# Second layer of a two-layer decoder on 1088 instead of 1104 columns: four slices of 272, no attention of the 16 meta queries, a residual tile of its own

## The chip, the cores and the metric

One Trainium2 chip, one core. The metric is the device time of one execution in microseconds (us). The core has a matrix engine (TensorE: PE, with its weight loads shown apart as PEld), a vector engine (VectorE: DVE), an engine for activation functions (ScalarE: ACT), a general engine (GpSimd: POOL) and a synchronising engine (SyncE: SP), which here does nothing but issue DMAs. Each engine runs its own instructions in program order and waits on semaphores for what the others make. A DMA issued from an engine stands in that engine's order too: where it must wait, everything behind it waits.

## The reference

One inference step of a decoder with two layers. Two groups of requests run through the same weights: one prompt of 1024 tokens, with 16 learned meta tokens ahead of it, and 8 samples of 8 new tokens each. The first layer is an mLSTM with state, the second an attention whose scores get a cumulative log-forget value per row (FoX). Keys, values and forget values come from the output of the first layer. Each layer is followed by a SwiGLU FFN (1024 to 2 x 2816 to 1024).

```
h = h + mlstm_mixer(rmsnorm(h, norm_a), ...);  h = h + swiglu(rmsnorm(h, norm_ffn[0]), ...)
k, v, lf = shared_kv(h, ...)                      # all 16 + 1024 rows of the prompt, 64 of the samples
h = h + fox_mixer(rmsnorm(h, norm_b), (k, v, lf)) # queries, gate, attention, w_out
h = h + swiglu(rmsnorm(h, norm_ffn[1]), ...)
y = rmsnorm(h, norm_final);   y_prompt = yp[:, N_META:]
```

Outputs are `y_prompt`, `y_sample`, the states and the keys, values and forget values (those of the meta tokens among them). Behind the keys and values the rows of the meta tokens reach no output: the last line drops them, and other rows' attention uses only their keys and values.

## The kernel before

**Columns.** The residual lies transposed: 1024 features as 8 blocks (`KT`) of 128 partitions, tokens as columns. There are `T` = 1104 columns: 64 of the samples (`NS`), 16 meta (`NM`), together `T0` = 80, and 1024 of the prompt. For the layers' large products they are cut into four slices `TS` of `SL` = 276 columns. Weights are the stationary operand, 128x128 each, and a slice streams past them. Every fp32 product is made of three matmuls (`mm3`, L193 to L195: high part by high, low part by high, high by low), so a 128x128 block against one slice is three matmuls of 276 columns.

**Stages of the second layer** (times in the profile):
- Sample attention, to about 1730 us: eight batches in `attend_sample` on POOL, ACT, DVE and PE. Between its small PE products stand the matmuls of the query gate (tile `bps`, 384 or 336 columns); `f(n)` puts n steps of them at a place. The order of PE is that of the code.
- The attention of the 16 meta queries, L2696 to L2731, behind the eighth batch: two groups of 8 heads. For each group SP issues 16 small loads of forget values (`nm`, `cm`), DVE adds the row mask `m16` to `nm`, POOL lays the queries out (`qmt`), PE makes the scores (`mps`, four matmuls), ACT the softmax, PE the transpose and the value products (`pom`), DVE the copy into `yS`. `m16` is made at the start of the kernel by `row_mask`.
- Prompt attention, `attend_prompt`, to 1978 us: scores `sp`, softmax, values, for 8 head pairs. The masks `nd` are made on POOL, and DVE's custom instruction adds them to the scores. Meanwhile the gate of the last head pair leaves as `ogb` to the DRAM tile `og2D`. `ys` and `first_tile` hold the 80 columns of samples and meta tokens.
- `mlp`: the output projection, `unit(t, m)` for four slices and 8 blocks m of 128 features: 24 matmuls into a PSUM tile `pops` (pool of four), then DVE adds it to the residual `Ht` (L535), then ACT squares it for the norm. The residual is loaded by SP from the DRAM tile `hD` (L499), slice by slice, among the loads of w_out (L518); DVE and ACT split the weights into high and low parts (`split`, L271 and L272).
- The FFN's first half: pairs of slices and of weight halves go through a Strassen-like scheme with seven products (`product`, L1650, tiles `m`), 22 units. DVE makes the sums and differences.
- The FFN's second half: seven rounds of down products (`dps`, L1989), then `Tail.finish` (L2116) and the final norm and transposes, `final` and `turn`.

**The norm.** `root` (L364) sums squares over partitions by tiny matmuls with one column: chunk by chunk of `NR` = 92 columns, three chunks, two tiles of squares each. A tiny fp32 matmul runs as two passes, so a root is 12 records of PE. ACT takes the root, `diag` (L375) makes a diagonal on DVE, `spread` (L382) spreads it over 128 partitions with one matmul of 276 columns. The second layer does this four times for the FFN's norm.

**What sets the order.** PE's order is that of the code throughout, DVE's and ACT's in the FFN as well; elsewhere a scheduler places DVE, ACT, POOL and SP instructions by their dependences. Many of the meta queries' loads are placed early: `nm` and `cm` stand among the loads of the first sample batches.

Of the kernel before, what the change touches and what calls it, by code (L numbers as in the profile page):

```python
# [32 lines left out]
SL = T // 4  # L33
NR = SL // 3
TS = [(SL * i, SL * i + SL) for i in range(4)]
# [10 lines left out]
NEG = -1.0e30  # L46

# [129 lines left out]
class Net:  # L177
# [19 lines left out]
    def consts(self):  # L197
        nc, I = self.nc, self.I
        c = self.ctx.enter_context(self.pool("const"))
        self.dram = self.ctx.enter_context(self.tc.tile_pool(name="scr", bufs=1, space=DRAM))  # L200
        self.c = c
        self.ident = c.tile([P, P], F32, name="ident")
        make_identity(nc, self.ident)
        self.ones = c.tile([P, P], F32, name="ones")
        nc.vector.memset(self.ones, 1.0)
        self.eps = c.tile([P, 1], F32, name="eps")
        nc.vector.memset(self.eps, EPS)
        self.gain = c.tile([P, NG], F32, name="gain")
        self.ptab = c.tile([1, NB * NPG], I32, name="ptab")
        self.clast = c.tile([P, 1], F32, name="clast")  # L210
        rm = c.tile([P, P], F32, name="rowm")
        self.q8, self.m16 = rm[:, :NQ], rm[:, NQ : NQ + NM]
        with self.pool("g0") as gp, self.pool("g0p", space=PSUM) as pp:
            rows = gp.tile([8, P], F32, name="grows")
            nc.scalar.dma_start(rows, I["norm_a"][0].rearrange("(k p) -> k p", p=P))
            nc.scalar.activation(self.clast, self.eps, AF.Sqrt)
            ps = pp.tile([P, 8], F32, name="gps")
            nc.tensor.transpose(ps, rows, self.ident[:8, :8])
            nc.vector.tensor_copy(self.gain[:, G_A : G_A + 8], ps)
# [106 lines left out]
    def place(self, nm):  # L326

        self.turn[nm] += 1
        a = ("ns", "nq", "nf").index(nm) * 2 * SL + self.turn[nm] % 2 * (SL if nm != "nf" else 4)
        return self.sq[:, a : a + (SL if nm != "nf" else 4)]  # L330

    def add_sq(self, H, t, m, sp, x, late=KT - 1):

        nc = self.nc
        t0, t1 = TS[t]
        n = t1 - t0
# [20 lines left out]
    def root(self, t, pp, **kw):  # L357

        nc = self.nc
        self.settle()  # L360
        ps = pp.tile([P, 512], F32, name=self.uid("nps"), **(kw or {"tag": "n"}))
        for c in range(3):
            for j, s in enumerate(self.sums[t]):
                nc.tensor.matmul(ps[:NR, c : c + 1], s[:, NR * c : NR * c + NR], self.ones[:, :1], start=j == 0,  # L364
                                 stop=j == 1)
        f = self.place("nf")[:NR]
        nc.scalar.activation(f[:, :3], ps[:NR, :3], AF.Sqrt, scale=1.0 / D, bias=self.eps[:NR])
        return [ps, f]

    def diag(self, st):  # L370

        nc, f = self.nc, st[1]
        nc.vector.reciprocal(f[:, :3], f[:, :3])
        d = self.place("nq")[:NR].rearrange("p (c n) -> p c n", c=3)
        nc.vector.tensor_tensor(out=d, in0=self.ident[:NR, :NR].unsqueeze(1).broadcast_to([NR, 3, NR]),  # L375
                                in1=f[:, :3].unsqueeze(2).broadcast_to([NR, 3, NR]), op=ALU.mult)
        st.append(d)

    def spread(self, st, r):

        nc, (ps, _, d) = self.nc, st
        nc.tensor.matmul(ps[:, :SL], self.ones[:NR], d.rearrange("p c n -> p (c n)"), start=True, stop=True)  # L382
        nc.scalar.copy(r, ps[:, :SL])

# [7 lines left out]
    def norm_jobs(self, H, t, g, r, pp=None):  # L392

        nc = self.nc
# [43 lines left out]
    def run(self):  # L438
# [6 lines left out]
        with ExitStack() as c1:  # L445
            xp = c1.enter_context(self.pool("x"))
            self.xs = [xp.tile([P, KT, PX + T], F32R, name=f"x{s}")[:, :, PX:] for s in "hl"]
            self.X, self.XG = ([tuple(x[:, :, a:b] for x in self.xs) for a, b in at] for at in (TS, TG))
            with ExitStack() as c2:
# [4 lines left out]
                H = [vt[:, KT * a : KT * b].rearrange("p (k n) -> p k n", k=KT) for a, b in TS]  # L454
# [6 lines left out]
            ys = yp.tile([P, KT, T0], F32, name="yS")  # L461
# [3 lines left out]
            cy.close()  # L465
            hp = c1.enter_context(self.pool("H"))
            self.H = hp.tile([P, KT, T], F32, name="Ht")
            H = [self.H[:, :, a:b] for a, b in TS]
            raws = [tuple(self.H[:, :, b : b + P] for b in (a, a + P)) for a in (0, 2 * P)]
            self.nr = hp.tile([P, SL], F32, name="nr")  # L470
            self.w2 = self.H[:, :2, :512]
            self.mlp(H, raws, I["w_out_b"][0], 1)

    def mlp(self, H, raws, w, l, heads=None, cb=None):

        nc = self.nc
        E = mybir.EngineType
        fixed, order = ExitStack(), ExitStack()
        self.sums = {}
        with self.pool(self.uid("nsp")) as sp, self.pool(self.uid("npp"), bufs=2, space=PSUM) as pn:  # L480
# [14 lines left out]
            with ExitStack() as c:  # L495
# [3 lines left out]
                load = lambda e, t: e.dma_start(H[t], self.hD[:, :, TS[t][0] : TS[t][1]])  # L499
# [26 lines left out]
                def unit(t, m, x):  # L526
# [10 lines left out]
                    if t % 2:  # L537
                        nc.gpsimd.dma_start(self.hD[:, m, TS[t][0] : TS[t][1]], H[t][:, m])
                    elif x == KT - 1:
                        nc.gpsimd.dma_start(self.hD[:, :, TS[t][0] : TS[t][1]], H[t])  # L540
# [77 lines left out]
    def turned(self, pool, nm):  # L618

        return {x: tuple(pool.tile([P, 4, SL], F32R, name=f"T{nm}_{x}{s}") for s in "hl") for x in (2, 1, 4)}  # L620
# [11 lines left out]
def values_a(self, v, kp, gates, w_in, c3):  # L632
# [9 lines left out]
    with ExitStack() as cw, self.pool("ppA0", bufs=4, space=PSUM) as pp:  # L642
# [205 lines left out]
        for n, dst in ((NQ, self.q8), (NM, self.m16)):  # L848
            self.row_mask(kp.tile([P, P // n, n], F32, name=self.uid("rm"), tag="rm"), dst, n)
# [751 lines left out]
def ffn(self, H, l, weights, order, TA, pn, pair, each, early, end=None):  # L1601
# [3 lines left out]
    nc, I = self.nc, self.I  # L1605
    E = mybir.EngineType
# [9 lines left out]
    with self.pool(f"ffn{l}") as fp, self.pool(f"ffnp{l}", space=PSUM) as pp:  # L1616
# [253 lines left out]
        with fixed(E.DVE, E.Activation):  # L1870
# [90 lines left out]
            for i, (hs, z, c) in enumerate(seq if each else seq[:-2]):  # L1961
# [18 lines left out]
                for m, h in [(m, h) for h in hs for m in range(4)] if apart else [(m, h) for m in range(4) for h in hs]:  # L1980
# [13 lines left out]
                    if last:  # L1994
# [3 lines left out]
                        if z in whole:  # L1998
                            t, y = whole[z]
                            if apart:  # L2000
                                square(2 * h + t - 1, 4 * y + m)
                                if m == 3:
                                    s = 2 * h + t - 1
                                    nc.scalar.dma_start(self.hD[:, :, TS[s][0] : TS[s][1]], H[s])
# [16 lines left out]
                for y, k in home[i] if i < len(home) else ():  # L2021
                    nc.gpsimd.dma_start(H[y][:, k : k + 2], self.hD[:, k : k + 2, TS[y][0] : TS[y][1]])
# [18 lines left out]
class Tail:  # L2041


    def __init__(self, net, fp, bank, pn, place):
        self.net, self.bank, self.pn = net, bank, pn
        self.at = TT[DONE[3][0]][0]
        self.sum = place[:, : T - self.at]
        self.last = net.slots[0][:, : T - self.at]
        self.tmp = [net.nr, fp.tile([P, SL], F32, name="tq")]
# [7 lines left out]
    def square(self, t, m, a=None, b=None, keep=False):  # L2057
        nc = self.net.nc
        a, b = a or max(TS[t][0], self.at), b or TS[t][1]
# [18 lines left out]
    def turn(self, ps, i, k):  # L2078
        self.net.nc.tensor.transpose(ps[:, k % 4 * P : k % 4 * P + P], self.net.H[:, k, slice(*TT[i])], self.net.ident)

    def second(self):
        nc = self.net.nc
        nc.vector.memset(self.last[:, : TS[3][0] - self.at], 0.0)
# [24 lines left out]
    def finish(self, acc, groups):  # L2108
        net = self.net
        nc, H = net.nc, net.H  # L2110
        for m in range(4):
            o = acc[m, 1][:, :SL]
# [4 lines left out]
            y = H[:, m, TS[3][0] :]  # L2117
# [14 lines left out]
def final(self, t, fp, pools):  # L2132

    nc, O = self.nc, self.O
    pp, pn = pools
# [371 lines left out]
def sample_masks(self, sp):  # L2507
# [15 lines left out]
    return dm, self.m16, qb  # L2523
# [23 lines left out]
def attend_sample(self, sk, sp, s2, pp, cq, ncn, masks, Y, fill):  # L2547
# [4 lines left out]
    dm, m16, qb = masks  # L2552
# [143 lines left out]
    vm = sp.tile([NM, D], F32, name="vmS", tag="vnS")  # L2696
    nc.sync.dma_start(vm, self.vD[:NM])
    for g in range(2):
        nm = sp.tile([P, NM], F32, name=f"nm{g}")
        cm = sp.tile([P, 1], F32, name=f"cm{g}")  # L2700
        for h in range(8):
            hh = 8 * g + h
            nc.sync.dma_start(nm[h * NM : (h + 1) * NM], self.cD[hh, :NM].partition_broadcast(NM))
            nc.sync.dma_start(cm[h * NM : (h + 1) * NM], self.cD[hh, :NM].unsqueeze(1))
        nc.vector.tensor_tensor(out=nm, in0=nm, in1=m16, op=ALU.add)
        Q = sp.tile([P, 4, P], F32, name=f"qmt{g}", tag="qmt")
        nc.gpsimd.memset(Q, 0.0)
        for j in range(4):
            for z in range(2):
                r = slice(z * 64, z * 64 + 64)  # L2710
                nc.gpsimd.tensor_copy(Q[r, j, (2 * j + z) * NM : (2 * j + z + 1) * NM], qt[r, 4 * g + j, NS:])
        pn = pp.tile([P, 512], F32, name=f"mps{g}", tag="sn", bufs=1)
        for j in range(4):
            nc.tensor.matmul(pn[:, :NM], Q[:, j, :], kt[:, 4 * g + j, NS:], start=(j == 0), stop=(j == 3))
        s = s2.tile([P, NM], F32, name=f"sM{g}", tag="sM")
        mx = s2.tile([P, 2], F32, name=f"mxM{g}", tag="mx")
        nc.vector.tensor_tensor_reduce(out=s, in0=pn[:, :NM], in1=nm, scale=1.0, scalar=NEG, op0=ALU.add,
                                       op1=ALU.max, accum_out=mx[:, 0:1])
        f(6)
        self.softmax_rows(s2, s, NM, mx[:, 0:1], cm, "S", 2)  # L2720
        nc.tensor.transpose(pn[:NM, 64 : 64 + P], s, self.ident)
        pt = s2.tile([NM, P], F32, name=f"ptM{g}", tag="ptM")
        nc.vector.tensor_copy(pt, pn[:NM, 64 : 64 + P])
        f(3)
        po = pp.tile([P, 4, 32], F32, name=f"pom{g}", tag="po", bufs=1)
        for j in range(4):
            nc.tensor.matmul(po[:, j, :], vm[:, (4 * g + j) * P : (4 * g + j + 1) * P], pt[:, j * 32 : j * 32 + 32],
                             start=True, stop=True)
        for z in range(2):
            r = slice(z * 64, z * 64 + 64)  # L2730
            nc.vector.tensor_copy(Y[r, 4 * g : 4 * g + 4, NS:T0], po[r, :, z * NM : z * NM + NM])  # L2731
# [11 lines left out]
def attend_prompt(self, ys):  # L2743
# [3 lines left out]
    with self.pool("ap", bufs=1) as sp, self.pool("ap2", bufs=2) as s2, self.pool("app", bufs=2, space=PSUM) as pp:  # L2747
# [25 lines left out]
        def first_tile():  # L2773

            og0 = w7f[1][:, : KT * T0].rearrange("p (k n) -> p k n", k=KT)
            nc.sync.dma_start(og0, self.og2D[:, :, :T0].rearrange("m p t -> p m t"))
            yield
            nc.vector.tensor_tensor(out=ys, in0=ys, in1=og0, op=ALU.mult)
            self.split(ys, *(x[:, :, :T0] for x in self.xs))
# [302 lines left out]
```

## Time and profile before

| | us |
|---|---|
| median of three runs | 2812.15 |
| lowest, highest | 2809.46, 2819.71 |
| the profiled run | 2814.68 |
| its span (first to last instruction) | 2813.1 |

The profiled run is 1.6 us longer than its span. The granted TensorE clock was 0.995 of full speed over the run.

The page gives busy time by engine, the span in 40 slices, and the costliest groups of instructions. A group's row is line, engine, operation, tile out<-tile in, shapes and count, then busy time, mean length, and idle time just before. Matmuls overlap: records of PE are longer than the step from one to the next. In rows by time the first number is the start in us from the span's start, the second the length; in square brackets stands how long the engine was idle before, and for whom. A window's row is its bounds and length, then busy time and instructions of the engines asked for, the granted clock, the DMA engines' share and GB/s.

The DMA engines by slices of 1/40 of the span (busy tenths, then GB/s):

```profile
DMA  7666555355564375545443775532524555527556
GB/s 214 174 184 175 154 158 196 108 154 157 175 177 137 119 248 172 189 146 166 145 167 131 257 278 207 170 128 87 158 86 130 176 176 162 162 91 233 185 190 220
```

### The profile page before, as it was taken

Reading aid. Unit: us, or ns where it says so; the run is one execution under the profiler, and the core shown is the slowest. Engines: PE = TensorE matmul, PEld = TensorE weight load, DVE = VectorE, ACT = ScalarE, POOL = GpSimd, SP = SyncE. Lnnn points to the kernel's source line nnn. Section 1 sums busy time; section 2 is a strip of 40 time slices with the busy share of each in tenths; the row PEclk is TensorE's granted clock in tenths of the full one; section 3 lists DMA queues with packets and bytes.
Section 4 is the critical chain, followed back from the end, with each engine's and each line's share of the span. In section 5 each row is a group of like instructions: output and inputs, shape, how many; then the busy total and the mean of one; then the engine's idle time right before and its main releaser. Section 6 shows DMA issues by size and latency. Waiting matters only on the chain. (4 is left out here: it accounts for less than half of the span.)

```text
span 2813.1 us, 60646 instructions
## 1 busy us (share of the span) xinstructions
PE 2751.4 (98%) x23543; PEld 2648.8 (94%) x23543; DVE 1793.8 (64%) x4025; ACT 1176.6 (42%) x2299; POOL 855.1 (30%) x1348
## 2 busy tenths in 40 slices
PE   9999989999999999999999999999999999999998
PEld 8999979999999999999999888677999999999998
DVE  5633556888887655662455444776388888765656
ACT  5432553422223334453444445777343223323345
POOL 3142333223223232124452202444313223323111
PEclk9999999999999999999999999999999999999999
DMA  7666555355564375545443775532524555527556
GB/s 214 174 184 175 154 158 196 108 154 157 175 177 137 119 248 172 189 146 166 145 167 131 257 278 207 170 128 87 158 86 130 176 176 162 162 91 233 185 190 220
DMA packets 432419, 474.05 MB, mean 169 GB/s; under 512 B 37014, under 2 KB 358290, under 8 KB 431106
## 3 DMA queue, kind: packets, MB, share of 16 engines
q1 hardware_dynamic: 380562, 320.52, 37.0%
q0 software_dynamic: 44928, 143.44, 15.5%
q10 hardware_dynamic: 6640, 6.21, 0.7%
q8 instruction: 185, 3.03, 0.5%
q14 instruction: 104, 0.85, 0.1%
HBM read 322.84 MB, written 147.21 MB: 167 GB/s over the span
## 5 line engine op out<-in xcount | busy, mean ns | idle before, releaser
L1650 PE MATMUL m<-xh,slot 128*128 128x276 f32 x2752 | 540.6, 290 | 1.9 <-ACT fs L1679 1.8
L1650 PEld LDWEIGHTS m<-xh,slot 128*128 128x128 f32 x2752 | 439.5, 188 | 3.8 <-ACT fs L1679 2.2
L1650 PE MATMUL m<-xl,slot 128*128 128x276 f32 x1376 | 397.0, 289 | 0.0
L1650 PEld LDWEIGHTS m<-xl,slot 128*128 128x128 f32 x1376 | 258.6, 188 | 0.0
L193 PE MATMUL tmps<-slot,xh 128*128 128x256 f32 (+2 forms) x864 | 243.1, 281 | 0.0
L195 PE MATMUL tmps<-slot,xl 128*128 128x256 f32 (+2 forms) x864 | 240.6, 278 | 0.0
L194 PE MATMUL tmps<-slot,xh 128*128 128x256 f32 (+2 forms) x864 | 240.5, 278 | 0.0
L272 DVE TENSOR_TENSOR slot<-slot,slot 128x1024 fp32r<-128x1024 f32 x124 | 162.8, 1313 | 60.7 <-ACT slot L271 59.2
L271 ACT CAST slot<-slot 128x1024 fp32r<-128x1024 f32 x124 | 129.5, 1045 | 143.9 <-PE m L1650 111.7
L194 PEld LDWEIGHTS tmps<-slot,xh 128*128 128x128 f32 (+1 forms) x864 | 159.2, 184 | 0.1
L195 PEld LDWEIGHTS tmps<-slot,xl 128*128 128x128 f32 (+1 forms) x864 | 158.6, 184 | 0.0
L193 PEld LDWEIGHTS tmps<-slot,xh 128*128 128x128 f32 (+1 forms) x864 | 158.4, 183 | 0.2
L193 PE MATMUL mmA<-xh,whi 128*128 128x384 f32 (+1 forms) x384 | 134.6, 350 | 2.9 <-ACT stg L960 2.9
L194 PE MATMUL mmA<-xl,whi 128*128 128x384 f32 (+1 forms) x384 | 128.9, 336 | 0.0
L195 PE MATMUL mmA<-xh,wlo 128*128 128x384 f32 (+1 forms) x384 | 128.7, 335 | 0.0
L272 DVE TENSOR_TENSOR slot<-vA,slot 128x1024 fp32r<-128x1024 f32 (+1 forms) x59 | 82.3, 1397 | 32.7 <-ACT slot L271 31.5
L272 DVE TENSOR_TENSOR slot<-Ht,slot 128x1024 fp32r<-128x1024 f32 (+1 forms) x59 | 82.0, 1393 | 32.7 <-ACT slot L271 31.6
L271 ACT CAST slot<-vA 128x1024 fp32r<-128x1024 f32 (+1 forms) x59 | 60.8, 1035 | 95.7 <-PE m L1650 90.7
L271 ACT CAST slot<-Ht 128x1024 fp32r<-128x1024 f32 (+1 forms) x59 | 60.9, 1036 | 95.5 <-PE m L1650 84.6
L1754 DVE TENSOR_TENSOR ws<-ws 128x128 f32<-128x128 f32 x264 | 93.8, 355 | 8.8
L2904 ACT ACTIVATE s<-s,nb 128x272 f32<-128x272 f32 (+7 forms) x126 | 98.8, 786 | 0.0
L2939 ACT COPY th<-tp 128x768 f32<-128x768 f32 (+1 forms) x80 | 73.5, 919 | 53.5 <-PE tp L2931 30.5
(809 smaller groups left out, 8675.1 us busy)
## 6 DMA issues: line engine op xcount, KB each, us to landing
ws<-in_w_down SPq DMA_DIRECT2D x176, 128.0 KB, 2.7
sD<-ws SPq DMA_DIRECT2D x176, 128.0 KB, 2.1
slot<-sD SPq DMA_DIRECT2D x40, 512.0 KB, 4.0
slot<-in_w_gate_up SPq DMA_DIRECT2D x36, 512.0 KB, 4.0
kp<-in_cache_k SPq DMA_DIRECT2D x32, 512.0 KB, 6.2
vp<-in_cache_v SPq DMA_DIRECT2D x32, 512.0 KB, 5.2
vA<-in_w_gate_up SPq DMA_DIRECT2D x26, 512.0 KB, 4.0
Ht<-in_w_gate_up SPq DMA_DIRECT2D x26, 512.0 KB, 3.9
```

Of the source, the lines that this page charges most:

```text
L193: mm(ps, sh, mh, start=first, stop=False)
L194: mm(ps, sh, ml, start=False, stop=False)
L195: mm(ps, sl, mh, start=False, stop=last)
L271: self.nc.scalar.copy(hi, src)
L272: self.nc.vector.tensor_tensor(out=lo, in0=src, in1=hi.bitcast(F32), op=ALU.subtract)
L1650: nc.tensor.matmul(u.ps[h, b], w[p][:, k], x[q][:, k], start=first and k == i == 0, stop=k == 3 and i == 2, skip_group_check=True)
L1754: tt(out=o, in0=a, in1=b, op=ALU.subtract)
L2904: nc.scalar.activation(ss[z, u], ss[z, u], AF.Exp, bias=nb[:, z : z + 1], accum_out=sm[:, u, z : z + 1])
L2939: nc.scalar.copy(th.rearrange("p x z (u h q) -> p h (x z u) q", h=2, q=64)[:, :, :n], pt[:, :, :n])
```

## The change

A class `Columns` holds the cuts of one layer, and the network holds the current one in `self.cols`. The first layer has 80 + 1024 columns as before (slices of 276, norm in 3 chunks of 92). The second has 64 + 1024 = 1088: slices of 272, norm in 4 chunks of 68. Its x is the same tile read from column 16 on, so the samples' 64 columns move up by 16 behind the keys and values. Its residual in SBUF is 1088 wide. In DRAM it gets a tile `hL`, which `mlp` writes and reloads; the first load still comes from `hD` by a new `load_h`, slice 0 in two pieces (64 and 208 columns), as the meta columns lie between. The loop over the meta queries, its row mask and its value load are deleted. `yS` and `first_tile` have 64 columns.

```diff
+class Columns:
+    def __init__(self, meta, x0):
+        self.T0 = NS + meta
+        self.T = self.T0 + SEQ
+        self.x0 = x0
...
+        self.SL = self.T // 4
+        self.NC = 4 if meta == 0 else 3
+        self.NR = self.SL // self.NC
+        self.TS = [(self.SL * i, self.SL * i + self.SL) for i in range(4)]
+LAYERS = (Columns(NM, 0), Columns(0, NM))
...
-        for c in range(3):
+        NR, NC = self.cols.NR, self.cols.NC
+        for c in range(NC):
             for j, s in enumerate(self.sums[t]):
                 nc.tensor.matmul(ps[:NR, c : c + 1], s[:, NR * c : NR * c + NR], self.ones[:, :1], start=j == 0,
                                  stop=j == 1)
...
+    def columns(self, l):
+        c = self.cols = LAYERS[l]
+        self.X = [tuple(x[:, :, c.x0 + a : c.x0 + b] for x in self.xs) for a, b in c.TS]
+        self.hL = self.hD if l == 0 else self.dram.tile([P, KT, c.T], F32, name="hL")
+    def load_h(self, e, H, t):
+        a, b = self.cols.TS[t]
+        x0 = self.cols.x0
+        if x0 and a == 0:
+            e.dma_start(H[0][:, :, :NS], self.hD[:, :, :NS])
+            a = NS
+        e.dma_start(H[t][:, :, a - self.cols.TS[t][0] :], self.hD[:, :, x0 + a : x0 + b])
...
-                load = lambda e, t: e.dma_start(H[t], self.hD[:, :, TS[t][0] : TS[t][1]])
+                load = lambda e, t: self.load_h(e, H, t)
...
-                        nc.gpsimd.dma_start(self.hD[:, m, TS[t][0] : TS[t][1]], H[t][:, m])
+                        nc.gpsimd.dma_start(self.hL[:, m, TS[t][0] : TS[t][1]], H[t][:, m])
...
-        for n, dst in ((NQ, self.q8), (NM, self.m16)):
-            self.row_mask(kp.tile([P, P // n, n], F32, name=self.uid("rm"), tag="rm"), dst, n)
+        self.row_mask(kp.tile([P, P // NQ, NQ], F32, name=self.uid("rm"), tag="rm"), self.q8, NQ)
...
-    vm = sp.tile([NM, D], F32, name="vmS", tag="vnS")
-    nc.sync.dma_start(vm, self.vD[:NM])
-    for g in range(2):
-        nm = sp.tile([P, NM], F32, name=f"nm{g}")
-        cm = sp.tile([P, 1], F32, name=f"cm{g}")
-        for h in range(8):
-            hh = 8 * g + h
-            nc.sync.dma_start(nm[h * NM : (h + 1) * NM], self.cD[hh, :NM].partition_broadcast(NM))
-            nc.sync.dma_start(cm[h * NM : (h + 1) * NM], self.cD[hh, :NM].unsqueeze(1))
-        nc.vector.tensor_tensor(out=nm, in0=nm, in1=m16, op=ALU.add)
...
-        f(6)
-        self.softmax_rows(s2, s, NM, mx[:, 0:1], cm, "S", 2)
...
-            nc.vector.tensor_copy(Y[r, 4 * g : 4 * g + 4, NS:T0], po[r, :, z * NM : z * NM + NM])
     for _ in fill:
         pass
```

What this moves is read from the instruction order of both kernels. A row is the line, the operation, out<-in with the tiles' numbers, the shape, and the semaphores that it waits for; line numbers of the changed kernel are larger by up to 37 for the same code.

PE at the end of the sample stage, before. `bps` is the gate, `mps` and `pom` are the meta queries' scores (here the transpose) and values, `sp` the prompt attention's first scores:

```order
L193 MATMUL bps_20575<-xh,slot_4993 128x384
L194 MATMUL bps_20575<-xl,slot_4993 128x384
L195 MATMUL bps_20575<-xh,slot_4994 128x384
L2721 MATMUL mps_20621<-ident,sM_20626 16x128 [waits Pool_49]
L2727 MATMUL pom_20655<-ptM_20653,vmS 128x32 [waits DVE_49]
L2727 MATMUL pom_20655<-ptM_20653,vmS 128x32 x3
L2877 MATMUL sp_1_0_0_20746<-kh_20716,qh_20709 128x144 [waits DMAHW7_49,DMAHW6_49,Activation_49]
L2877 MATMUL sp_1_0_1_20747<-kh_20716,qh_20709 128x144 [waits Activation_49]
```

The same place in the changed kernel:

```order
L206 MATMUL bps_20470<-xh,slot_4935 128x384
L207 MATMUL bps_20470<-xl,slot_4935 128x384
L208 MATMUL bps_20470<-xh,slot_4936 128x384
L2878 MATMUL sp_1_0_0_20582<-kh_20552,qh_20545 128x144 [waits DMAHW6_49,DMAHW5_49,Activation_49]
L2878 MATMUL sp_1_0_1_20583<-kh_20552,qh_20545 128x144 [waits Activation_49]
```

The last gate matmul is followed by the first score. All 42 gate matmuls that stood among the meta products are still there, in the same order.

DVE between two sample batches, before. `slot` is a gate weight being scaled and cast, `kT` and `ptS` are copies for the samples' keys and probabilities, `od` and `o` make a batch's output:

```order
L2589 COPY kT_18644<-ktp_18645 128x512 [waits PE_49]
L2625 COPY ptS_18663<-spn_18544 64x128 [waits PE_49]
L266 SCALAR_TENSOR_TENSOR slot_4991<-slot_4985,gain,slot_4987 128x128 [waits DMAHW7_49,PE_49,Activation_49]
L2705 TENSOR_TENSOR nm_20509<-nm_20509,rowm 128x16 [waits DMAHW5_49,DMAHW7_49,DMAHW3_49,DMAHW1_49]
L2637 SCALAR_TENSOR_TENSOR od_18715<-po_18694,nb_18556,dm 128x256 [waits DVE_49,PE_49]
L2640 TENSOR_REDUCE o_18717<-od_18715 128x64 [waits DVE_49]
```

And in the changed kernel:

```order
L2626 COPY kT_18586<-ktp_18587 128x512 [waits PE_49]
L2662 COPY ptS_18605<-spn_18486 64x128 [waits PE_49]
L279 SCALAR_TENSOR_TENSOR slot_4933<-slot_4927,gain,slot_4929 128x128 [waits DMAHW7_49,PE_49,Activation_49]
L2674 SCALAR_TENSOR_TENSOR od_18657<-po_18636,nb_18498,dm 128x256 [waits DVE_49,PE_49]
L2677 TENSOR_REDUCE o_18659<-od_18657 128x64 [waits DVE_49]
```

The add that waited for four DMA queues is gone; its neighbours stand as before.

SP at the start of the output projection, before. `slot` and `woraw` are raw blocks of w_out, `Ht` the residual's slices:

```order
L518 DMA slot_25351<-in_w_out_b 128x8x128 [waits DMAHW0_49]
L518 DMA woraw_25370<-in_w_out_b 128x8x128 [waits DMAHW1_49,PE_49,Activation_49]
L518 DMA woraw_25371<-in_w_out_b 128x8x128 [waits DMAHW2_49,DVE_49]
L518 DMA woraw_25372<-in_w_out_b 128x8x128 [waits DMAHW3_49]
L499 DMA Ht<-hD 128x8x276 [waits DVE_49,DMAHW4_49,PE_49,DMAHW6_49,Activation_49,Pool_49]
L518 DMA woraw_25369<-in_w_out_b 128x8x128 [waits DMAHW5_49]
```

And in the changed kernel:

```order
L553 DMA slot_25188<-in_w_out_b 128x8x128 [waits DMAHW7_49]
L553 DMA woraw_25207<-in_w_out_b 128x8x128 [waits DMAHW0_49,PE_49]
L553 DMA woraw_25208<-in_w_out_b 128x8x128 [waits DMAHW1_49,PE_49,Activation_49]
L553 DMA woraw_25209<-in_w_out_b 128x8x128 [waits DMAHW2_49]
L504 DMA Ht<-hD 128x8x64 [waits DVE_49,DMAHW3_49,PE_49,DMAHW5_49,Activation_49,Pool_49]
L506 DMA Ht<-hD 128x8x208 [waits DMAHW4_49]
L553 DMA woraw_25206<-in_w_out_b 128x8x128
```

The residual's first slice comes in two pieces, behind the same five weight loads. The three `woraw` loads took their places in SBUF from other tiles: before from the prompt attention's last probabilities and values (their PE and ACT instructions end at its end), now from tiles of scores and probabilities that the last head pairs finish before that.

102 lines of the change are left out of this document (43 added, 59 removed).

## The prediction

> **What bounds the kernel now.** I read the busy table first, then the chain of waits, then busy time by stage.
>
> ```profile
> span 2813.1 us, 60646 instructions
> PE 2751.4 (98%) x23543; PEld 2648.8 (94%) x23543; DVE 1793.8 (64%) x4025; ACT 1176.6 (42%) x2299; POOL 855.1 (30%) x1348
> PE 35%; DVE 4%; issue 2%; ACT 2%; DMA 1%; SPq 0%; POOL 0%; DVEq 0%; ACTq 0%; POOLq 0%
> 1715.00:1730.00 15.00, 14.43 (x98) 12.97 (x93) 4.09 (x18) 7.37 (x11) 4.98 (x19) 1.00 0.78 277
> 1730.00:1978.00 248.00, 232.35 (x3173) 175.44 (x3172) 169.68 (x833) 187.66 (x381) 118.29 (x297) 1.00 0.40 133
> 1978.00:2100.00 122.00, 121.06 (x956) 119.76 (x956) 76.52 (x130) 43.77 (x76) 33.29 (x40) 1.00 0.45 135
> 2100.00:2470.00 370.00, 366.50 (x2878) 365.18 (x2878) 305.78 (x564) 113.22 (x177) 106.70 (x71) 1.00 0.53 156
> 2470.00:2805.00 335.00, 333.26 (x2621) 331.35 (x2619) 212.66 (x347) 135.94 (x228) 74.11 (x109) 1.00 0.58 187
> ```
>
> After the stretch a row gives PE, PEld, DVE, ACT, POOL busy (with instructions), the granted clock, the DMA share and GB/s. The five rows are the end of the sample attention, the prompt attention (unchanged), the second layer's output projection, its FFN up, its FFN down. PE is 98% busy and heads the chain, at full clock: in the second layer what counts is how far apart matmuls start. DVE comes next, 305.78 of 370 us in the FFN.
>
> **A: narrower matmuls.** How many are there? The windows of the second layer for products (L1650), down rounds (L1989), the tail (L2116) and the output projection (tile pops), PE and PEld busy:
>
> ```profile
> 1977.50:2813.10 835.60, 471.39 (x3696) 469.29 (x3696) 1.00 0.54 166
> 1977.50:2813.10 835.60, 230.59 (x1800) 229.29 (x1800) 1.00 0.54 166
> 1977.50:2813.10 835.60, 6.61 (x48) 6.20 (x48) 1.00 0.54 166
> 1977.50:2813.10 835.60, 100.38 (x768) 98.17 (x768) 13.61 (x32) 1.00 0.54 166
> ```
>
> 3696 + 1800 + 48 + 768 = 6312 matmuls, 276 columns each, 272 after the change. What do four columns cost? No row shows the change itself, but stretches in which PE never idles show the step of several widths. A matmul's record is about 0.29 us long (0.34 at 384 columns), the step less, because they overlap; so step = (stretch + 0.29 us) / count. PE alone, in the order 276, 272, 272, 256, 256, 384 columns:
>
> ```profile
> 2150.00:2250.00 100.00, 100.00 (x789) 1.00 0.56 166
> 1265.20:1292.00 26.80, 26.80 (x216) 1.00 0.49 165
> 52.00:69.00 17.00, 17.00 (x137) 1.00 0.33 60
> 75.00:115.00 40.00, 40.00 (x356) 1.00 0.69 195
> 1243.00:1265.00 22.00, 22.00 (x188) 1.00 0.33 107
> 181.00:188.80 7.80, 7.80 (x47) 1.00 0.87 283
> ```
>
> Steps: 127.1 (a count of 790 would make it 126.9, which I use), 125.4, 126.2, 113.1, 118.6, 173.1 ns. Bounds of the gain per matmul: 126.9 - 126.2 = 0.7 ns, and 4/20 of the way to the lower 256-column step, (126.9 - 113.1)/5 = 2.8 ns. I take 126.9 - 125.4 = 1.5 ns, since the 272-column stretch at 1265 us is the longer one and, like the second layer, streams x against weights prepared in slots; the line from 256 to 384 columns, 60/128 = 0.47 ns a column, gives 1.9 ns. A = 6312 x 1.5 = **-9.5 us** (-4.4 to -17.4).
>
> The Trainium skill, "TensorE: Matmul & The Clock Gate", section "Back-to-back issue gap", gives two figures for the spacing of load-and-matmul pairs: a sustained one, about 81 ns at 128 columns and 131 at 512, and an isolated one, N/2.4 + 2.5 ns. I estimate from them 0.52 and 1.67 ns for four columns, so 3.3 or 10.5 us. The trace disagrees with the sustained one: 173.1 ns at 384 columns is above its 131 at 512. The isolated slope is near the 1.5 ns.
>
> **B: the 16 meta queries at the end of the sample stage.** PE by time, then the gate matmuls among it (tile bps, all engines):
>
> ```profile
> 1716.78 0.27 PE L2645 MATMUL po<-ident,o 128*64 128x128 f32 x1
> 1716.88 0.96 PE L2714 MATMUL mps<-ktS,qmt 128*128 128x16 f32 x8
> 1717.69 0.42 PE L193 MATMUL bps<-xh,slot 128*128 128x384 f32 x1
> 1729.46 0.34 PE L2877 MATMUL sp<-kh,qh 64*128 64x144 f32 x2
> 1716.90:1729.40 12.50, 8.06 (x43) 7.15 (x42) 0.98 (x2) 1.00 0.89 324
> ```
>
> From the first meta product (1716.88) to the first prompt score (1729.46) are 12.58 us. PEld counts 42 gate matmuls there, which stay: 42 x 173.1 ns = 7.27 us. The rest, meta matmuls and waits between them, goes: B = **-5.3 us**. At most 5.3; at least the 0.9 us that the eight meta products alone take, if something else is late at once.
>
> **C: a wait in the sample stage.** The 32 small loads of nm and cm stand in SP's queue among the cache and weight loads, and the add that needs them stands in DVE's order between two sample batches:
>
> ```profile
> 1596.13 0.18 DVE L2705 TENSOR_TENSOR nm<-nm,rowm 128x16 f32<-128x16 f32 x1 [4.83 <-DMA nm<-cD]
> 1596.15 0.34 PE L195 MATMUL bps<-xh,slot 128*128 128x384 f32 x1
> 1599.95 0.67 PE L193 MATMUL bps<-xh,slot 128*128 128x384 f32 x1
> 1704.49 0.27 PE L2645 MATMUL po<-ident,o 128*64 128x128 f32 x1
> 1705.39 0.42 PE L193 MATMUL bps<-xh,slot 128*128 128x384 f32 x1
> ```
>
> DVE stood 4.83 us. Gates covered PE until 1596.15 + 0.173 = 1596.32; the next gate came at 1599.95, 3.63 us later, with only the sample products between. In an undisturbed batch the same piece takes 1705.39 - 1704.49 = 0.90 us. C = 0.90 - 3.63 = **-2.7 us**; nothing if the next weight cast is late there, as its load stood behind the same queue.
>
> **D: start of the output projection.**
>
> ```profile
> 1990.45 1.15 DVE L535 TENSOR_TENSOR Ht<-Ht,pops 128x276 f32<-128x276 f32 x3 [1.57 <-DMA Ht<-hD]
> 1982.04 1.03 SPq L499 DMA_DIRECT2D Ht<-hD  x1
> PE pops L193 <- DVE Ht L535: 0.5, 1, 0.5
> PE pops L195 <- DVE wo L272: 0.2, 1, 0.2
> ```
>
> The fifth unit waits for a PSUM bank, freed by an add which waits for the residual. Three weight loads stood ahead of that load in SP's queue and waited for the prompt attention's last products; in the new order they wait for earlier ones, so the residual starts earlier. Both waits go, with the 0.3 us that PE needs to fill again: D = **-1.0 us**, between 0 and -1.6 (DVE's wait). Splitting slice 0 into 64 and 208 columns adds one issue, 1.03 us as the row of SP has it; what covers it is the earlier start, and without that it would lengthen the wait by as much.
>
> **E: four chunks in the norm's root.** Twelve passes become sixteen in each of four roots. The group of L364 in the second layer, then one root by time:
>
> ```profile
> L364 PE MATMUL nps<-ones,sq 128*92 128x1 f32 x48 | 4.3, 216 | 0.2 <-DVE sq L349 0.2
> 2007.06 1.06 PE L364 MATMUL nps<-ones,sq 128*92 128x1 f32 x12
> 2007.98 0.37 PE L193 MATMUL pops<-xh,slot 128*128 128x276 f32 x1
> ```
>
> 48 passes become 64. From the root's first pass to the next matmul are 0.92 us, 77 ns a pass: E = 16 x 77 ns = **+1.2 us**; at most 16 x 216 ns, the length of one record, = 3.5, and nothing if a gap that is there anyway takes them.
>
> **F: the attention's first mask.** The last gate's result leaves by POOL before the masks:
>
> ```profile
> 1729.35 0.58 POOL L2404 DMA_DIRECT2D og2D<-ogb  x1 [1.60 <-ACT ogb L2403]
> 1730.10 2.83 POOL L2847 TENSOR_TENSOR nd<-ncb,mneg 128x256 f32<-128x256 f32 x4
> 1730.88 0.35 DVE L2881 CUSTOM_DVE_ANT_0 s<-sp,nd,mxf 128x128 f32<-128x128 f32 x1 [0.64 <-POOL nd L2847]
> ```
>
> DVE already waits 0.64 us for the mask. With the meta products gone, the scores follow the last gate directly, while ACT and POOL need as long as before: F = **+0.6 us**, from 0 to 1.6 (POOL's wait).
>
> **G: DVE in the FFN's first rounds.**
>
> ```profile
> 2100.00:2110.00 10.00, 8.12 (x62) 7.80 (x61) 8.44 (x17) 4.88 (x8) 0.00 (x0) 1.00 0.27 77
> 2130.00:2140.00 10.00, 9.14 (x73) 8.92 (x72) 9.79 (x21) 3.04 (x6) 3.09 (x3) 1.00 0.36 110
> ```
>
> Here PE loses 1.9 and 0.9 us to DVE. DVE's adds shorten with the columns, 4 in 276, its weight casts don't. A counts 62 to 73 x 1.5 = 0.1 us in each such 10 us; where DVE sets the pace, over some 40 us, that is given back: G = **+0.4 us** (0 to +0.5).
>
> At nothing: POOL's row mask at the start and its query copies, ACT's two softmaxes, SP's other loads. They lie under PE rows that are full. The second residual tile writes and reads the same bytes less 1.4%, under the same products. If such cover were gone it would be a fraction of a microsecond each.
>
> **Sum.** -9.5 - 5.3 - 2.7 - 1.0 + 1.2 + 0.6 + 0.4 = -16.3 us. The profiled run took 2814.68 us (span 2813.1 and 1.6 around it), 2.5 over the median of 2812.15, and should come to 2798.4. On the median: 2812.15 - 16.3 = **2795.9 us**.
>
> **Rivals.**
>
> 1. *The weight loads set the step, not the columns.* For: PEld is busy 365.18 of PE's 366.50 us in the FFN, and a load is 128 columns before and after. Against: 256 and 384 columns step 113.1 and 173.1 ns with the same loads. Then A is nothing and the sum -6.8: 2805.4 us. The Trainium skill's sustained figures, cited above, point this way.
> 2. *The step to 272 is as steep as the one to 256.* For: 113.1 ns; against: 125.4 and 126.2. A = -17.4, the sum -24.2: 2788.0 us.
> 3. *Freed waits are taken by the next one* at B and C: the edits do what they say, but a weight cast or the scores' loads are late at once. DMA at 0.89 of its share in B's stretch speaks for it, the two clean neighbours against. -16.3 + 5.3 + 2.7 = -8.3, and 2803.9 us.
> 4. *Slower: the 272-column stream falls into a worse pattern.* The step depends on more than width: 256 columns step 113.1 ns in one place, 118.6 in another, at full clock in both. If 272-column reads in the second layer, from a start 16 columns in, met such a penalty, the step would be 125.4 + 5.5 = 130.9 ns, 4.0 over today: +25.2 - 6.8 = +18.4, so 2830.6 us. It decides from 6.8 us / 6312 = 1.1 ns, a step of 128.0. Against: both 272-column rows lie below that.
>
> **How the numbers follow.** Forecast, with A anywhere from -4.4 to -12: 0.72; rival 1: 0.08; rival 2: 0.10; rival 3: 0.06; rival 4: 0.04. A measurement of this kernel can tell about 0.5%, 14 us, from no change; the line is 2798.1 us. The forecast's 2795.9 lies 2.2 us below it, which A keeps to down to -7.3, so of its 0.72 I put 0.52 below the line and 0.20 above. Faster: 0.52 + 0.10 = 0.62. Same: 0.20 + 0.08 + 0.06 = 0.34. Slower: 0.04. The range runs from a little below rival 2, 2786, to a little above rival 1, 2808; rival 4 stays out.
>
> **What would show it.** A: 272-column stretches with some 799 matmuls per 100 us (125.4 ns); 789 again is rival 1, 807 rival 2, under 782 rival 4. B: gates follow one another to the first score, in 7.3 us. C: no DVE wait for nm, and the piece between gates at 0.9 us. D: no wait of pops for Ht. E: 64 root passes in the second layer, 1.23 us from a root's first pass to the next matmul. F: DVE's first wait for nd at about 1.2 us instead of 0.64. The prediction fails if the prompt attention, 248 us with untouched code, changes its length by over 2 us, for which I have no term.

## The result and the profile after

| | before | after |
|---|---|---|
| median (5 runs each), us | 2813.53 | 2796.92 |
| lowest to highest, us | 2809.46 to 2819.71 | 2794.96 to 2798.37 |
| the profiled run, its span, us | 2814.68, 2813.1 | 2798.37, 2796.5 |

The ratio of the times is 0.9937, with a 95% interval of 0.9921 to 0.9952. The medians lie 16.6 us apart, and so do the two spans. The same parts of the page as before, after the change: totals, chain, then the five stages (sample stage's end, prompt attention, output projection, FFN up, FFN down; their bounds are moved with the work):

```profile
span 2796.5 us, 60483 instructions
PE 2736.1 (98%) x23525; PEld 2635.6 (94%) x23525; DVE 1786.7 (64%) x4008; ACT 1169.0 (42%) x2291; POOL 848.6 (30%) x1304
PE 36%; DVE 4%; ACT 2%; issue 2%; POOL 0%; DMA 0%; DVEq 0%; ACTq 0%; POOLq 0%
1708.00:1723.00 15.00, 14.63 (x113) 12.54 (x114) 2.08 (x8) 3.30 (x5) 1.61 (x3) 1.00 0.48 171
1723.00:1971.00 248.00, 232.26 (x3171) 175.57 (x3170) 169.20 (x829) 187.55 (x381) 118.48 (x298) 1.00 0.43 139
1971.00:2093.00 122.00, 120.76 (x980) 119.78 (x981) 78.20 (x132) 45.49 (x80) 32.48 (x40) 1.00 0.41 121
2093.00:2454.00 361.00, 358.85 (x2844) 357.27 (x2843) 299.05 (x556) 108.75 (x172) 106.62 (x71) 1.00 0.54 159
2454.00:2788.50 334.50, 332.80 (x2648) 331.18 (x2647) 214.03 (x352) 136.56 (x229) 74.33 (x109) 1.00 0.57 187
```

PE is 98% busy and heads the chain as before; its work has become shorter by 15.3 us. To see where, I took the same DVE and ACT instructions in both traces and subtracted their start times; the difference grows by these steps:

| place | us | terms of the prediction |
|---|---|---|
| up to 1550 us, the same code but for POOL's row mask | -0.6 | none |
| sample stage, 1550 to 1700 | -2.1 | C -2.7 |
| its end and the first scores | -4.4 | B -5.3, F +0.6 |
| prompt attention, rest | +0.2 | none |
| first projection matmul to last matmul | -9.6 | A -9.5, D -1.0, E +1.2, G +0.4 |
| behind it | -0.1 | none |
| sum | -16.6 | -16.3 |

The rows of the changed kernel that answer to those of the terms, in this order: PE's step, columns 272 (A); PE at the sample stage's end and DVE's first mask (B, F); the gates around `po` (C); DVE's first residual add (D); one root and the matmul behind it (E).

```profile
2250.00:2350.00 100.00, 100.00 (x796) 1.00 0.58 172
1714.07 0.27 PE L2682 MATMUL po<-ident,o 128*64 128x128 f32 x1
1721.56 0.33 PE L2878 MATMUL sp<-kh,qh 64*128 64x144 f32 x1
1722.26 0.33 PE L2878 MATMUL sp<-kh,qh 64*128 64x144 f32 x1 [0.37 <-ACT ogb L2440]
1723.98 0.35 DVE L2882 CUSTOM_DVE_ANT_0 s<-sp,nd,mxf 128x128 f32<-128x128 f32 x1 [1.03 <-POOL nd L2848]
1597.40 0.27 PE L2682 MATMUL po<-ident,o 128*64 128x128 f32 x1
1598.30 0.42 PE L206 MATMUL bps<-xh,slot 128*128 128x384 f32 x1
1981.69 1.13 DVE L570 TENSOR_TENSOR Ht<-Ht,pops 128x272 f32<-128x272 f32 x3 [3.22 <-DMA Ht<-hD]
1998.66 1.09 PE L378 MATMUL nps<-ones,sq 128*68 128x1 f32 x16
1999.61 0.37 PE L206 MATMUL pops<-xh,slot 128*128 128x272 f32 x1
```

The step, worked out as in the prediction: 100.29 / 796 = 126.0 ns by this row. The distances from one start to the next, with those over 150 ns (waits) left out, average 125.55 ns over layer 2, and 126.88 before: 1.33 ns a matmul. The meta stretch, 12.68 us from `po` to the first score, is 7.49; the mask wait grew from 0.64 to 1.03, and PE waits 0.37 for the last gate's activation. Between the gates stand 0.90 us instead of 3.63. DVE waits 3.22 us for the residual, but PE no longer does. A root takes 0.95 us, 0.92 before.

**The clock.** Part of the difference in the sample stage is clock. In every trace of this case the granted clock is halved now and then, for 3.41 us or a small multiple of it. The rows show PE in the 3.41 us before such a stretch and in the stretch, first in the kernel before, then in the changed one; the last row is the changed kernel at the work of the second. Behind the counts stands the granted clock:

```profile
1595.36:1598.77 3.41, 1.68 (x10) 1.00 0.49 136
1598.77:1602.18 3.41, 3.41 (x15) 0.50 0.90 330
1567.01:1570.43 3.42, 1.29 (x11) 1.00 1.03 314
1570.43:1573.85 3.42, 3.42 (x24) 0.50 1.01 299
1599.00:1603.00 4.00, 4.00 (x68) 1.00 1.00 339
```

By the starts of the work behind them, the half clock costs some 1.0 us in the second row and 1.5 in the fourth. With both taken out the sample stage gained 2.6 us instead of 2.1.

Both stretches follow waits of PE, so the halved clock can't simply be set apart from the kernels. The one before follows the stall of term C, and it comes again at 1598.64 us in the one other trace with the old sample stage (the run with the residual first, below); so C is worth up to 3.7 us there. The one of the changed kernel follows a wait of PE of 2.5 us for `kT` (2.4 us before, with no halving behind it). It is there in the five traces without the 32 small loads, near 1570 us, and in none of the six with them. The waits for `kT` are of like length in both groups, 2.1 to 3.2 us and 1.9 to 3.1, so its 1.5 us may be a price of the change. What decides it is open.

### The profile page after: what moved, and what is told of

Same layout as the page of the kernel before. It is cut to its first block, busy times and chain, and to the rows that moved or that the text cites. A ratio compares the mean times of both kernels' runs of the same rounds, so it can differ in the third digit from the quotient of the medians.

```text
span 2796.5 us, 60483 instructions
## 1 busy us (share of the span) xinstructions
PE 2736.1 (98%) x23525; PEld 2635.6 (94%) x23525; DVE 1786.7 (64%) x4008; ACT 1169.0 (42%) x2291; POOL 848.6 (30%) x1304
## 5 line engine op out<-in xcount | busy, mean ns | idle before, releaser
L1685 PE MATMUL m<-xh,slot 128*128 128x276 f32 (+1 forms) x2752 | 539.1, 289 | 2.0 <-ACT fs L1714 2.0
L1685 PE MATMUL m<-xl,slot 128*128 128x276 f32 (+1 forms) x1376 | 396.7, 288 | 0.0
```

The lines of the kernel that those rows point to most:

```text
L1685: nc.tensor.matmul(u.ps[h, b], w[p][:, k], x[q][:, k], start=first and k == i == 0, stop=k == 3 and i == 2, skip_group_check=True)
```

## The experiments

**Width and meta attention apart.** These are two halves of the change: first the deleted attention without the width, then the width without the deletion.

```diff
-LAYERS = (Columns(NM, 0), Columns(0, NM))
+LAYERS = (Columns(NM, 0), Columns(NM, 0))
...
-            self.split(ys, *(x[:, :, NM:T0] for x in self.xs))
+            self.split(ys, *(x[:, :, :NS] for x in self.xs))
```

> The changed kernel with the second layer back on 1104 columns (slices of 276, norm in 3 chunks of 92); the meta attention stays away, so the 16 meta columns of layer 2 carry leftover x and reach no output. My theory (terms B, C, D, F of the prediction are apart from the width): the step in layer 2 is back at 126.9 ns, the piece between the gates in the sample stage is 0.9 us, the stretch from the last po to the first prompt score is about 7.5 us, PE does not wait for Ht at the fifth unit, and the time is about 8 us below the kernel before (ratio 0.9971). Rival (the freed waits come back elsewhere, all of the gain is width): within 2 us of the kernel before. Rival on D (the early residual comes from the narrower residual tile): PE waits for Ht again, as before, 0.5 us and a weight wait of 0.2.

Measured: 2806.19 us (median) against 2812.13, ratio 0.9976, interval 0.9967 to 0.9986: 6.7 us by the ratio, 5.9 between the medians. The first row is PE's step with 276 columns, the second the only wait of PE that the waits view has between 1971 and 2100 us:

```profile
2250.00:2350.00 100.00, 100.00 (x790) 1.00 0.58 171
PE m L1685 <- ACT fs L1714: 0.9, 1, 0.9
```

The step is the old one, the gain of the attention is there, and PE waits neither for `Ht` nor for weights, though the residual is 276 wide. So the rival on D falls: D doesn't come from the narrower residual.

For the second half the deleted lines and the mask are put back and `yS` is 80 columns wide:

```diff
-            ys = yp.tile([P, KT, NS], F32, name="yS")
+            ys = yp.tile([P, KT, T0], F32, name="yS")
...
+    for g in range(2):
+        nm = sp.tile([P, NM], F32, name=f"nm{g}")
...
```

> The changed kernel with the attention of the meta queries put back (its 16 columns are then not used; yS is 80 columns wide again). My theory: layer 2 steps at 125.5 ns as in the changed kernel, the root passes stay 64, the nm wait of DVE (4 to 5 us) and the 12 us stretch at the end of the sample stage are back, and the time is 8 us below the kernel before (6312 x 1.32 = 8.3 for the step, plus 1.2 for the roots, less about 1 from a stall of the FFN that is gone), ratio about 0.997. On D: the three weight loads wait for the end of the attention again, so PE waits for Ht again, some 0.5 us. Rival (weight loads set the step and the 8 us came from elsewhere): step 126.9 ns and the time within 2 us of the kernel before.

Measured: 2803.99 us, ratio 0.9968, interval 0.9956 to 0.9981: 9.0 us by the ratio, 8.1 between the medians. PE's step, the wait for weights in the projection, the residual's first add, and the meta stretch's two ends:

```profile
2250.00:2350.00 100.00, 100.00 (x796) 1.00 0.57 169
PE pops L208 <- DVE wo L285: 0.9, 2, 0.7
1989.65 1.13 DVE L570 TENSOR_TENSOR Ht<-Ht,pops 128x272 f32<-128x272 f32 x3 [1.32 <-DMA Ht<-hD]
1715.44 0.96 PE L2752 MATMUL mps<-ktS,qmt 128*128 128x16 f32 x8
1728.04 0.33 PE L2916 MATMUL sp<-kh,qh 64*128 64x144 f32 x2
```

The step is that of the changed kernel and the 12.6 us are back. DVE's waits for `nm` are back too, 5.0 us in two, but the piece between the gates takes 1.51 us and not 3.63. From the first projection matmul to the last matmul it took 818.6 us, 827.0 before, 817.4 with the whole change: width and roots are worth 8.4. The two halves, 6.7 and 9.0, add to 15.7; their intervals are too wide to tell that from the whole, 16.6. PE waits again, but for a weight, not for `Ht` as I had expected.

**What the early weight loads need.** As the run before, but the meta queries' outputs go to a tile of their own and `yS` is back at 64 columns:

```diff
-            ys = yp.tile([P, KT, T0], F32, name="yS")
+            ys = yp.tile([P, KT, NS], F32, name="yS")
...
+    ym = sp.tile([P, KT, NM], F32, name="yM")
```

> The kernel of e2_narrow_with_meta with yS back at 64 columns; the meta queries' outputs go to a small tile of their own in the sample stage's pool (nothing reads it). My theory of D (yS's 16 columns decide at which addresses the three raw weight tiles lie, and so whose end they wait for; the width of the residual and the meta attention have no part in it): the three loads run some 15 us ahead of the projection, the residual lands about 6.5 us behind its issue instead of over 8, PE waits neither for Ht nor for wo in the first units, and from the first projection matmul to the last matmul there is 1 to 1.4 us less than in e2_narrow_with_meta. Rival (the early loads need the meta attention gone): the loads wait for the attention's end and PE waits 0.5 to 1.5 us as in e2_narrow_with_meta.

Measured: one run of 2800.70 us, 2812.53 before. SP's last two early loads, the residual's first issue, and its first add:

```profile
1960.48 0.99 SPq L553 DMA_DIRECT2D woraw<-in_w_out_b  x2
1977.93 0.54 SPq L504 DMA_DIRECT2D Ht<-hD  x1
1984.14 1.13 DVE L570 TENSOR_TENSOR Ht<-Ht,pops 128x272 f32<-128x272 f32 x3 [2.88 <-DMA Ht<-hD]
```

The loads run 17 us ahead of the residual's issue, the residual lands 6.2 us behind its issue, PE has no wait of `pops`, and layer 2 takes 817.2 us, 1.4 less. Nothing but where the 16 columns are kept differs: D hangs on the width of `yS`, which moves what is allocated behind it. Its size is less sure: the run with the loads alone, below, has the changed kernel's layer 2 and its early weight loads, and takes 818.4 us. The first add starts 7.5 us behind the residual's issue there, PE waits 0.3 us for weights in the projection, and most of the rest is a wait in the FFN's second half. In the eight traces with early loads that add starts 6.1 to 7.5 us behind the issue, in the two with late loads ahead of the residual 7.8 to 8.4.

**The residual ahead of the loads.** The kernel before, with one load moved:

```diff
-                        if m in (4, 6, 7):
-                            for t in (0,) if m == 4 else (1,) if m == 6 else (2, 3):
+                        if m in (1, 6, 7):
+                            for t in (0,) if m == 1 else (1,) if m == 6 else (2, 3):
```

> The kernel before with the residual's first slice placed in SP's order ahead of the three weight loads that stood before it. My theory of D (the residual's issue waits for the end of the attention in any case, 4.2 us behind the first projection matmul in both kernels; what the change brought is that these three loads, 1.5 MB, no longer share the DMA engines with it): the residual lands some 2 us sooner, PE's wait of 0.5 us for Ht is gone, but the weights come later: PE waits 1 to 4 us for wo at the units behind. Rival (the residual is simply late by the queue): both waits gone, 1 us gained.

Measured: one run of 2821.47 us, 2814.92 before. SP's issue, the add on DVE, PE's waits in the projection's first 22 us, and PE in a stretch of half clock behind the first wait:

```profile
1982.01 0.54 SPq L499 DMA_DIRECT2D Ht<-hD  x1
1987.93 0.44 DVE L535 TENSOR_TENSOR Ht<-Ht,pops 128x276 f32<-128x276 f32 x1 [6.54 <-DMA Ht<-hD]
PE pops L193 <- ACT slot L271: 6.1, 1, 6.1
PE pops L195 <- DVE slot L272: 0.4, 1, 0.4
1987.76:1994.59 6.83, 3.59 (x14) 0.50 1.21 290
```

The issue doesn't move: 4.2 us behind the first projection matmul, as in all these kernels. The residual lands 5.9 us behind it instead of 8.4, since the three loads no longer share the DMA engines. But the weights behind come so late that PE waits 6.5 us, more than I had expected, and the clock is halved for the last of the wait and 4 us of the work behind it. Some 7 us are lost.

**The wait in the sample stage.** The changed kernel with the loads and the adds on `nm`, then with the loads alone:

```diff
...
+        for h in range(8):
+            hh = 8 * g + h
+            nc.sync.dma_start(nm[h * NM : (h + 1) * NM], self.cD[hh, :NM].partition_broadcast(NM))
+            nc.sync.dma_start(cm[h * NM : (h + 1) * NM], self.cD[hh, :NM].unsqueeze(1))
+        nc.vector.tensor_tensor(out=nm, in0=nm, in1=m16, op=ALU.add)
...
```

> The changed kernel with only the 32 small loads of nm and cm and the two adds on nm put back (their results are not used; no scores, softmax or values of the meta queries). My theory of C (the add waits in DVE's order for loads that wait in SP's queue, and the sample products behind it wait): DVE waits 4 to 5 us for nm, the piece between the gates is 3.6 us instead of 0.9, everything behind it is 2.7 us later than in the changed kernel, apart from clock episodes of about 1.5 us each. Rival (the stall was the clock or the page loads): the piece stays at 0.9 us.

> As the run before, but the 32 loads alone, without the adds on DVE (nothing reads them). My theory (the waiting add is what costs, since it stands in DVE's order): no DVE wait for nm, the piece between the gates is 0.9 us, no loss against the changed kernel above the 1.5 us of a clock episode. Rival (the 32 issues on SP delay the page and weight loads behind them, about 9 us of SP's queue): PE or DVE waits 1 to 3 us for kp, vp, nck or a gate weight in the sample stage instead.

Measured: one run each of 2801.82 and 2798.38 us. The first three rows are of the kernel with adds (DVE's wait, PE's pass and the next gate), the next two of that with the loads alone:

```profile
1598.46 0.18 DVE L2741 TENSOR_TENSOR nm<-nm,rowm 128x16 f32<-128x16 f32 x1 [3.48 <-DMA nm<-cD]
1600.01 0.27 PE L2683 MATMUL po<-ident,o 128*64 128x128 f32 x1
1601.73 0.42 PE L206 MATMUL bps<-xh,slot 128*128 128x384 f32 x1
```

```profile
1596.20 0.27 PE L2682 MATMUL po<-ident,o 128*64 128x128 f32 x1
1597.10 0.42 PE L206 MATMUL bps<-xh,slot 128*128 128x384 f32 x1
```

With the add the wait is back and the piece takes 1.72 us; without it, 0.90. So the add makes the stall, as expected, but a smaller one than the 3.6 us that I had expected: a wait of 3.48 us costs 0.8 here, while 4.83 cost 2.7 before. The gates cover the first part. Over the whole sample stage, and with the changed kernel's 1.5 us of halved clock taken out, loads and adds cost 2.7 us and the loads alone 0.9. In the first, PE waits 0.7 us for a page of keys that SP issued behind them (0.3 in the second), so the rival has a share too.

**Narrower still.** Slices of 268 and of 256 in layer 2. These kernels leave the last 16 and 64 prompt tokens out of layer 2's projection and FFN:

```diff
-        self.SL = self.T // 4
+        self.SL = self.T // 4 if meta else 268
...
```

> The changed kernel with slices of 268 in layer 2: the last 16 prompt tokens are left out of layer 2's output projection and FFN (their residual is zero). My theory (the step follows the columns by about 0.33 to 0.42 ns each): step 123.9 to 124.2 ns in the FFN, layer 2 about 8 to 10 us shorter than in the changed kernel. Rival (weight loads set it, 276 to 272 was something else): 125.5 ns.

> The changed kernel with slices of 256 in layer 2: the last 64 prompt tokens are left out of layer 2's output projection and FFN (their residual is zero). My theory (a line in the columns, 1/2.4 ns each, from 125.5 at 272): step about 118.9 ns, the 118.6 of the first layer's 256-column stretch at 1243 us of the kernel before. Rival 2 of the prediction (256 columns are steeper, 113.1 ns as at 75 us): about 113. Rival 1 (weight loads): 125.5 ns.

Measured: one run each of 2794.29 and 2775.20 us (the first lost some 3 us in the prompt attention, which is the same code, with the clock halved from 1792.1 to 1798.9 us). PE in 100 us of the FFN with 268 and one of its waits there, then both for 256:

```profile
2250.00:2350.00 100.00, 99.60 (x804) 1.00 0.58 173
PE m L1686 <- ACT Ht L1715: 0.7, 3, 0.3
```

```profile
2250.00:2350.00 100.00, 97.61 (x812) 1.00 0.58 174
PE m L1686 <- ACT Ht L1715: 2.5, 7, 0.5
```

Without waits the steps average 123.47 ns (268) and 118.88 (256). With 125.55 and 126.88 that is 8.0 ns over 20 columns, 0.40 each; for four of them 1.3 between 276 and 272, 2.1 between 272 and 268. Weight loads as the bound would have left all four alike. But in the rows PE is no longer full: it waits in every second unit at 268, 0.2 to 0.5 us, and in nearly every one at 256, up to 0.65, most of it between the first and the second product, which share a bank: ACT must copy the first out (L1715, `m1_out`) before the second goes on in it. From 272 to 268 the steps give 6312 x 2.08 = 13.1 us, and layer 2 got 8.6 shorter, 817.4 to 808.8. In the changed kernel one such wait (0.2 us by the waits view) is there already, in the kernel before none.

**The root's passes.**

```diff
-        self.NC = 4 if meta == 0 else 3
+        self.NC = 8 if meta == 0 else 3
```

> The changed kernel with the norm's root of layer 2 in eight chunks of 34 instead of four of 68: 32 passes a root instead of 16, 128 in all. My theory of E (passes stand on PE's path at 77 ns each): from a root's first pass to the next matmul 2.46 us instead of 1.23, and layer 2 4.9 us longer than in the changed kernel. Rival (the passes fall into gaps that are there anyway, or a narrow pass is shorter): under 2 us longer.

Measured: one run of 2799.78 us. One root and the matmul behind it:

```profile
1996.88 1.23 PE L378 MATMUL nps<-ones,sq 128*34 128x1 f32 x32
1998.03 0.39 PE L206 MATMUL pops<-xh,slot 128*128 128x272 f32 x1
```

32 passes take 1.16 us, not 2.46. From most passes to the next are 33 ns at 34 columns of squares, 62 at 68, 82 at 92: the price of a pass goes with the columns that are loaded, so cutting 272 into more pieces adds little to the roots. Layer 2 took 820.5 us, 3.1 more than with four chunks, and the roots explain 0.8 of it. The step was 0.2 ns longer in that run, which makes 1.4; I can't say why, and the rest is open. So neither my 4.9 us nor the rival's "under 2" holds for the whole layer.

## Why the prediction was right, step by step

2795.9 us were forecast and 2796.92 measured, and the mechanism of the main terms is shown; the sum is better than its parts.

- **A**, -9.5: right in kind, a little large. The steps are 126.88 and 125.55 ns, 1.33 instead of 1.5: -8.4. Both stand-ins were within 0.15 ns (126.9 and 125.4), but what counts is their difference, and a tenth of a nanosecond is 0.6 us here.
- **B and F**, -4.7: -4.4 in the two profiles. All 42 gate matmuls now close up, and the mask's wait takes back some 0.4 us on DVE and 0.4 on PE.
- **C**, -2.7: the piece between the gates is as forecast (0.90), and putting the add back brought the stall back. Its size isn't fixed: 2.7 us in the two traces of the old sample stage, 0.6 to 0.8 in the three where the add was put back into the changed kernel (1.51, 1.61 and 1.72 us for the piece), since it is what is left of DVE's wait when the gates run out. The queue behind the 32 issues is worth up to 0.9 more. The prediction had no term for the clock: half clock behind the stall cost 1.0 us before, another such stretch costs the changed kernel 1.5, and that the two nearly cancel is luck.
- **D**, -1.0: right in size, 1.1 in the two profiles and 1.4 in the experiment (with a scatter of 1.2 between runs of the same layer 2), and wrong in one link. "So the residual starts earlier" doesn't hold: it is issued 4.2 us behind the first projection matmul in both. It lands earlier, 6.5 us behind its issue instead of 8.4, because 1.5 MB of weights had been moved before. The split into two pieces costs nothing that shows.
- **E**, +1.2: mis-sized. I gave a pass of 68 columns the price of one of 92. A root takes 0.953 us instead of 0.925: +0.1.
- **G**, +0.4: not borne out. Of the four stalls of 1.1 to 1.3 us in FFN's first rounds one is gone and another grew by 0.4; the waits of layer 2, apart from D's, add up to 11.9 us before and 11.7 after.
- **Rivals.** 1 (weight loads set the step) and 4 (a worse pattern) fall with the steps at 276, 272, 268 and 256. 2 (as steep as 113.1 ns at 256) falls too: in layer 2 256 columns step 118.9 ns, like the stretch at 118.6 that also reads its weights from slots. 3 (the next wait takes the gain) holds for a part of C only. The sustained figures of the Trainium skill, "TensorE: Matmul & The Clock Gate", section "Back-to-back issue gap", don't fit: 0.13 ns a column against 0.40 here. Its isolated slope, 1/2.4 = 0.42, does.

The gain of A was set 1.1 us too high and the losses of E and G 1.5 us too high; that these cancelled is luck.

## What to carry to other kernels

Where PE is full, what a narrower matmul gives is the difference of two steps, and steps are read from full stretches of both widths, not from lengths of records. Deleting a small piece of work between full engines gives back its waits as well, and these are to be looked for on every engine that its instructions stand in line on: a small add that waits for a load stalls all that is behind it. And when a tile shrinks, what is allocated behind it moves, and with it what the next loads wait for: that is read from the instruction order, before any time is known.

## What was not expected of the hardware

- The granted clock halves for 3.41 us or a small multiple at a time, and this goes with PE's waits. The stretches near 1570 us (five traces) and 1599 us (two) each follow 3.41 us in which PE was 20% to 50% busy. It is no strict rule: PE was 46% and 49% busy over 3.41 us near 1570 us in two runs (the loads alone, the width without the deletion) and the clock stayed full, and other stretches, at 165, 1726 and 1792 us, follow a PE that was 72% busy or more. Two of the experiments have the same code ahead of the sample stage, and one was 3.6 us ahead at 500 us; its clock had been halved for 6.8 us up to there, that of the other for 23.9. The rows of PE between 350 and 425 us, first of the width without the deletion, then of the one with `yS` at 64 columns:

```profile
350.00:425.00 75.00, 66.54 (x509) 0.91 0.52 163
350.00:425.00 75.00, 63.87 (x521) 0.98 0.57 183
```

  The clock differs, 0.91 and 0.98. That may be a good part of the 10 us between lowest and highest before, which no run tests. It is a reason to compare stages, not spans, where less than some 5 us is in question.
- A matmul with one moving column is priced by its stationary side: 33, 62 and 82 ns from most to the next at 34, 68 and 92 columns.
- The copy of the first product out of its bank is next in line: it leaves PE full at 276 columns, shows once at 272, in every second unit at 268 and in nearly every one at 256.
